# Column sums in 32-column tiles, roots spread by transposes, merge pairs in one PSUM bank, and single-tile stores at the end

## The chip, the cores and the metric

The kernel runs on one core of one Trainium2 chip. Its time is the device time of one execution in microseconds (us). Three runs of the kernel before took 1862.31, 1863.15 and 1863.52 us, a median of 1863.15 us. TensorE does the matrix products, VectorE the element work, ScalarE activations and copies, GpSimd a little of both; the SyncE queue issues the transfers. In the rows of the profile these are PE (with PEld for its weight loads), DVE, ACT, POOL and SP.

## The reference, cut to what matters

A sequence of 512 positions with 1024 features (fp32) goes through two blocks. Every layer starts with a norm over the features and adds its result to the stream `x`; in the first block the result of a layer is normed as well before it is added.

```python
def rmsnorm(x, g):
    return x * lax.rsqrt(jnp.mean(x * x, axis=-1, keepdims=True) + EPS) * g

# block 1
h = rmsnorm(x, norm_mix_pre); proj = h @ w_in
merged = sigmoid(g_a) * pool_mixer(u_pool) + sigmoid(g_b) * conformer_conv(u_glu)
x = x + rmsnorm(merged @ w_o, norm_mix_post)
f = square(relu(rmsnorm(x, norm_mlp_pre) @ w_up)) @ w_down
x = x + rmsnorm(f, norm_mlp_post)
# block 2
h = x + deltanet_mixer(rmsnorm(x, a_norm))      # 8 heads, chunks of 64, a triangular solve in each
h = h + conv_ffn(rmsnorm(h, f_norm[0]))
h = h + swa_sink_attention(rmsnorm(h, b_norm), kv)   # window 128, 16 heads
h = h + conv_ffn(rmsnorm(h, f_norm[1]))
return rmsnorm(h, final_norm)
```

## The kernel before

The stream lies in SBUF as 8 tiles of 128 features by 512 positions. Each big product is cut into blocks of 128x128 weights times 128x512; weights and inputs are split into a rounded fp32r part and a remainder, so that a block is three matmuls (`mm3`, L277 to L279). The weights come in units of 512 KB on the SyncE queue, ScalarE rounds them (L253) and VectorE forms the remainder (L254).

A norm needs the sum of squares over all features at each position. Features lie on partitions, so the squares of the 8 tiles are added up into one tile `sq`, and TensorE adds its 128 partitions: `colsum` (L341) takes each of the four 128-column blocks of `sq` as weights against a column of ones. The sums of 128 positions then stand on 128 partitions, one column for each block. `rms` (L373) scales them, takes the root by an integer guess and three Newton steps (`rsqrt`, L324, eleven small VectorE instructions with that scaling), and `bcast` (L348) spreads the four columns of roots along partitions again: VectorE multiplies the identity by each column (L352, four 128x128 diagonal matrices `dg`), and one matmul with ones (L355) writes the 128x512 result. `rms` is called seven times.

At three places a layer is handed to the next in two halves of the positions: between the mixer and the MLP of block 1, between that MLP and the delta layer, and from the last FFN to the final norm. `lin_split` (L405) computes the last 24 blocks of the outgoing product for the first 256 positions and then for the others, and `half_rms` (L436) is the norm of one half: two column sums (L440), the same root chain (L443, then L327 to L333), two diagonals (L447) and a 128x256 matmul (L449). `fold` (L427) adds the squares of each finished half tile to `sq`: ScalarE squares (L433), VectorE adds (L434). `begin` (L452) takes both halves' results `R`, updates the stream and splits it for the next product, and the first products of the next layer fill TensorE there. `final` (L1334) multiplies the halves by the roots (L1346, eight instructions of 128x256 a half) and stores pairs of tiles, 256 KB each, on the SyncE queue.

In the delta layer the heads' 64x64 triangular inverses are joined from 32x32 quarters for four heads at a time (`delta_merge`, L840, groups 0 and 1). One quarter step is many 32x32 or 64x64 matmuls that use only a part of the array: L867 first, then L882 with L883 into two PSUM tiles `p` and `r`, L888 into `r`, and for pairs of heads `left` (L898) into `pl` and `right` (L902) into `pr`; `right` needs the copy `M` of what `left` made of the same heads. These steps are woven between the blocks of other products (`weave`, L297).

The order on each engine is set by a scheduler at build time, from the order of the program, priorities and the tiles that are free. Each engine works its instructions strictly in that order. PSUM has eight banks: six or three for `acc`, two or five for `aux`, by stage.

Of the kernel before, what the change touches and what calls it, by code (L numbers as in the profile page):

```python
# [74 lines left out]
def _pack(i):  # L75
# [43 lines left out]
    for g, w in enumerate(WINDOWS):  # L119
        cnt[:, g * 16:g * 16 + w] = 1.0 / np.arange(1, w + 1, dtype=np.float32)  # L120
    a["cnt"] = cnt
# [69 lines left out]
class Net:  # L191
# [149 lines left out]
    def colsum(self, x):  # L341
        ps = self.aux()
        for b in range(NB):
            self.nc.tensor.matmul(ps[:, b:b + 1], lhsT=x[:, b * P:(b + 1) * P], rhs=self.ones[:, 0:1],
                                  start=True, stop=True)
        return ps[:, :NB]

    def bcast(self, y, copy=True):  # L348
        nc = self.nc
        dg = self.tmp()  # L350
        for b in range(NB):
            nc.vector.tensor_scalar(out=dg[:, b * P:(b + 1) * P], in0=self.ident, scalar1=y[:, b:b + 1],  # L352
                                    scalar2=None, op0=ALU.mult)
        ps = self.aux()
        nc.tensor.matmul(ps, lhsT=self.ones, rhs=dg, start=True, stop=True)  # L355
# [17 lines left out]
    def rms(self, acc, n, copy=True):  # L373
        v = self.small()
        self.nc.vector.tensor_scalar(out=v, in0=self.colsum(acc), scalar1=1.0 / n, scalar2=EPS,
# [60 lines left out]
    def half_rms(self, sq, i):  # L436
        nc = self.nc
        ps, h = self.aux(), S // 2
        for j in range(2):
            nc.tensor.matmul(ps[:, j:j + 1], lhsT=self.blk(sq, 2 * i + j), rhs=self.ones[:, 0:1],  # L440
                             start=True, stop=True)
        v = self.small(2)
        nc.vector.tensor_scalar(out=v, in0=ps[:, 0:2], scalar1=1.0 / D, scalar2=EPS, op0=ALU.mult, op1=ALU.add)  # L443
        y = self.rsqrt(v)
        dg = self.tmp()
        for j in range(2):
            nc.vector.tensor_scalar(out=self.blk(dg, j), in0=self.ident, scalar1=y[:, j:j + 1], scalar2=None,  # L447
                                    op0=ALU.mult)
        nc.tensor.matmul(ps[:, h:], lhsT=self.ones, rhs=dg[:, :h], start=True, stop=True)  # L449
        return ps[:, h:]  # L450

    def begin(self, gain, heads=()):  # L452
# [8 lines left out]
        for i in range(2):  # L461
            next(steps, None)
            R.append(self.half_rms(sq, i))
# [376 lines left out]
    def delta_merge(self, g):  # L840
# [38 lines left out]
        p, r = self.aux(), self.aux()  # L879
        for i in range(n):  # L880
            c = slice(i * Q, (i + 1) * Q)
            T.matmul(p[q[0], c], lhsT=TTq[q[1], i], rhs=Mq[q[1], i], start=True, stop=True)  # L882
            T.matmul(r[q[2], c], lhsT=Mq[q[3], i], rhs=TTq[q[3], i], start=True, stop=True)  # L883
        for k, t in enumerate(T64):
            A.copy(out=t[q[1], :, 0:Q], in_=half(cq(p)[q[0]], k))
        yield
        for i in range(n):
            T.matmul(r[q[0], i * Q:(i + 1) * Q], lhsT=Mq[q[1], i], rhs=TTq[q[1], i], start=True, stop=True)  # L888
        for i, s in enumerate(hs):
            for k, f in ((0, A.copy), (2, V.tensor_copy)):  # L890
                f(out=s["t4"][q[k], :, q[k + 1]], in_=cq(r)[q[k], i * NB:(i + 1) * NB])
# [12 lines left out]
        for h in range(0, GROUP + 2, 2):  # L904
            pl, pr = (self.aux() if h < GROUP else None), (self.aux() if h else None)
            for i in range(2 * NB):
                if h < GROUP:
                    left(h, i, c64(pl))
                if h:
                    right(h - 2, i, c64(pr))  # L910
            if h < GROUP:
                M = self.hid()
                A.copy(out=M[bot], in_=pl[top])
                Ms[h] = c64(M)
            if h:
                for i in range(2):
                    V.tensor_copy(out=hs[h - 2 + i]["t4"][top, :, bot], in_=c64(pr)[bot, i * NB:(i + 1) * NB])
# [188 lines left out]
    def ffn(self, i):  # L1106
# [23 lines left out]
        if i:  # L1130
            sq = self.tp.tile([P, S], F32, tag="sq", name=self.name("sq"), bufs=2)
# [6 lines left out]
            self.carry = self.lin_split(st, NH, hs, done), sq  # L1138
# [195 lines left out]
    def final(self):  # L1334
        nc = self.nc
        steps, sq = self.carry
# [55 lines left out]
```

## Time and profile before

| | |
|---|---|
| median of three runs | 1863.15 us |
| the profiled execution | 1860.65 us |
| its span, first to last instruction | 1858.7 us |
| mean granted TensorE clock | 0.992 |
| PE busy | 1825.9 us, 98% |
| DVE busy | 1232.8 us, 66% |
| ACT busy | 821.9 us, 44% |
| POOL busy | 94.3 us, 5% |
| DMA, mean over the span | 95 GB/s |

The durations below come from the profiled execution, whose time is 1.95 us over its span and 2.5 us under the median. A row of the timeline gives the start, how long the instruction or the run of like instructions lasted, engine, line, operation and operands. Matmuls overlap: a 128x512 block product lasts 0.39 us and the next starts 0.227 us after it, so that costs on TensorE are read from starts, not from durations. A column sum has its `sq` block as weights; a matmul of fp32 data shows as two records, a transpose as one.

### The profile page before, as it was taken

The numbers are of one execution on the slowest core, as the hardware profiler recorded it, in microseconds if no ns is written. First come the engines' busy times: TensorE is split into PE (matmuls) and PEld (weight loads), VectorE is DVE, ScalarE is ACT, GpSimd is POOL, SyncE is SP. The second block draws the span as 40 slices with busy tenths as digits, with TensorE's granted clock in tenths as the row PEclk, the third lists the DMA queues.
The fourth block names the chain that finished last, engine by engine and source line by source line (L and its number), as shares of the span: only waits on it lengthen the run. The fifth ranks groups of instructions, "written<-read, shape, count | busy, mean of one in ns | idle before, by whom it ended". The sixth has DMA issues, their size and how long they took to land.

```text
span 1858.7 us, 24170 instructions
## 1 busy us (share of the span) xinstructions
PE 1825.9 (98%) x9214; PEld 1517.8 (82%) x9214; DVE 1232.8 (66%) x2323; ACT 821.9 (44%) x1447; POOL 94.3 (5%) x225
## 2 busy tenths in 40 slices
PE   8999999999999999999999999999999999999997
PEld 6887898888888878787878888888877788888887
DVE  7999767423543887968687777633577777777334
ACT  5323443222332477755454444422377644444221
POOL 0000000000000026430000000000000000000000
PEclk9999999999999999999899999999999999999999
DMA  5322223323232322325123232222211222223221
GB/s 181 102 91 93 95 69 102 102 91 102 91 103 91 125 81 86 117 83 170 36 80 102 92 101 93 100 97 96 97 58 57 69 91 92 102 93 100 96 97 57
DMA packets 62676, 175.70 MB, mean 95 GB/s; under 512 B 15200, under 2 KB 17888, under 8 KB 62560
## 3 DMA queue, kind: packets, MB, share of 16 engines
q1 hardware_dynamic: 62560, 174.16, 28.3%
q8 instruction: 72, 1.18, 0.3%
q14 instruction: 44, 0.36, 0.1%
HBM read 166.80 MB, written 7.34 MB: 94 GB/s over the span
## 4 chain that ended last, share of the span: by engine, by line
PE 91%; DVE 7%; ACT 1%; issue 1%; DMA 0%; DVEq 0%; ACTq 0%
PE m L277 28%; PE m L278 28%; PE m L279 27%; DVE wl L254 1%; PE a L627 1%; PE a L1315 1%; PE a L641 1%; PE a L1255 1%; DVE t L616 1%; PE a L1308 1%; PE a L935 0%; DVE xl L312 0%; DVE h L1239 0%; PE a L355 0%; PE a L941 0%
## 5 line engine op out<-in xcount | busy, mean ns | idle before, releaser
L277 PE MATMUL m<-xh,wh 128*128 128x512 f32 (+1 forms) x1560 | 602.1, 389 | 10.9 <-ACT xh L311 6.6
L278 PE MATMUL m<-xl,wh 128*128 128x512 f32 (+1 forms) x1560 | 599.6, 385 | 0.6
L279 PE MATMUL m<-xh,wl 128*128 128x512 f32 (+1 forms) x1560 | 599.8, 385 | 0.2 <-DVE wl L254 0.2
L253 ACT CAST wh<-wr 128x1024 fp32r<-128x1024 f32 x302 | 317.0, 1051 | 570.7 <-PE m L278 473.6
L254 DVE TENSOR_TENSOR wl<-wr,wh 128x1024 fp32r<-128x1024 f32 x302 | 368.7, 1222 | 244.9 <-ACT wh L253 241.9
L277 PE MATMUL m<-h,wh 128*128 128x512 f32 (+1 forms) x972 | 360.8, 372 | 3.1 <-ACT h L308 2.3
L278 PE MATMUL m<-h,wh 128*128 128x512 f32 (+1 forms) x972 | 359.6, 370 | 0.0
L279 PE MATMUL m<-h,wl 128*128 128x512 f32 (+1 forms) x972 | 359.3, 370 | 0.0
L277 PEld LDWEIGHTS m<-xh,wh 128*128 128x128 f32 x1560 | 292.4, 189 | 71.8 <-ACT xh L311 9.4
L278 PEld LDWEIGHTS m<-xl,wh 128*128 128x128 f32 x1560 | 294.3, 189 | 59.4 <-DVE xl L312 2.5
L279 PEld LDWEIGHTS m<-xh,wl 128*128 128x128 f32 x1560 | 294.1, 189 | 57.6 <-issue 0.7
L277 PEld LDWEIGHTS m<-h,wh 128*128 128x128 f32 x972 | 183.6, 189 | 35.6 <-issue 3.1
L278 PEld LDWEIGHTS m<-h,wh 128*128 128x128 f32 x972 | 183.7, 189 | 30.9 <-issue 1.8
L279 PEld LDWEIGHTS m<-h,wl 128*128 128x128 f32 x972 | 183.6, 189 | 30.5 <-issue 0.6
L1119 DVE SCALAR_TENSOR_TENSOR t<-t,vecs,t 128x511 f32<-128x511 f32 (+1 forms) x176 | 131.2, 747 | 5.3 <-ACT t L1117 2.4
L1116 DVE TENSOR_TENSOR t<-m,R 128x512 f32<-128x512 f32 x88 | 60.5, 688 | 79.9 <-PE m L279 77.7
L308 ACT CAST h<-t 128x512 fp32r<-128x512 f32 x80 | 49.6, 621 | 139.6 <-DVE t L1127 115.1
L501 DVE SCALAR_TENSOR_TENSOR h<-h,vecs,h 128x511 f32<-128x511 f32 (+28 forms) x120 | 82.5, 731 | 0.9 <-ACT h L498 0.9
L309 DVE TENSOR_TENSOR h<-t,h 128x512 fp32r<-128x512 f32 x80 | 55.1, 689 | 28.4 <-ACT h L308 28.2
L1117 ACT ACTIVATE t<-t,vecs 128x512 f32<-128x512 f32 x88 | 71.5, 813 | 2.0 <-DVE t L1116 1.7
L1125 ACT ACTIVATE t<-t 128x512 f32<-128x512 f32 x44 | 27.8, 632 | 84.2 <-DVE t L1119 84.2
L583 DVE TENSOR_TENSOR t<-m,R 128x512 f32<-128x512 f32 x32 | 22.1, 690 | 58.6 <-PE m L279 56.7
(269 smaller groups left out, 1534.6 us busy)
## 6 DMA issues: line engine op xcount, KB each, us to landing
wr<-in_f_up SPq DMA_DIRECT2D x88, 512.0 KB, 3.5
wr<-in_f_down SPq DMA_DIRECT2D x44, 512.0 KB, 3.5
wr<-in_w_up SPq DMA_DIRECT2D x32, 512.0 KB, 3.5
wr<-in_w_down SPq DMA_DIRECT2D x32, 512.0 KB, 3.4
wr<-in_a_w_in SPq DMA_DIRECT2D x32, 512.0 KB, 3.5
wr<-in_w_in SPq DMA_DIRECT2D x28, 512.0 KB, 3.5
wr<-in_w_o SPq DMA_DIRECT2D x8, 512.0 KB, 3.5
spill<-h SPq DMA_DIRECT2D x16, 256.0 KB, 2.3
```

The costliest lines, as they stand in the source:

```text
L253: nc.scalar.copy(out=wh, in_=raw)
L254: nc.vector.tensor_tensor(out=wl, in0=raw, in1=wh.bitcast(F32), op=ALU.subtract)
L277: nc.tensor.matmul(ps, lhsT=w[0], rhs=x[0], start=start, stop=False)
L278: nc.tensor.matmul(ps, lhsT=w[0], rhs=x[1], start=False, stop=False)
L279: nc.tensor.matmul(ps, lhsT=w[1], rhs=x[0], start=False, stop=stop)
L308: nc.scalar.copy(out=hi, in_=src)
L309: nc.vector.tensor_tensor(out=lo, in0=src, in1=hi.bitcast(F32), op=ALU.subtract)
L501: nc.vector.scalar_tensor_tensor(out=c[:, d:], in0=v[:, :S - d], scalar=wt[CONV_K - 1 - d], in1=c[:, d:], op0=ALU.mult, op1=ALU.add)
L1116: V.tensor_tensor(out=u, in0=ps, in1=R, op=ALU.mult)
L1117: A.activation(out=y, in_=u, func=AF.Identity, scale=w[2], bias=self.vec(f"f_b{i}", c))
L1119: V.scalar_tensor_tensor(out=y[:, d:], in0=u[:, :S - d], scalar=w[2 - d], in1=y[:, d:], op0=ALU.mult, op1=ALU.add)
L1125: A.activation(out=g, in_=g, func=AF.Silu)
```

## The change

`colsum` takes each 128-column block as four tiles of 32 columns: 16 matmuls of 128x32 weights in place of four of 128x128, each writing its own 32 partitions of the result. It may also add up several input tiles. `spread` is new and replaces the diagonals and the matmul with ones: the column of roots, read as if repeated 128 times, is transposed by TensorE, one 128x128 transpose for each block of positions. Both serve `rms` and `half_rms`.

`root` is new and used by `half_rms` alone: ScalarE takes the square root of the scaled sum (L345 of the new program), VectorE inverts it (L347) and does one Newton step (L348 to L350). `rms` keeps `rsqrt`. In `delta_merge` the matmuls of `p` and `r` in the first step, and those of `left` and `right`, write different partitions of one PSUM tile; the copies move accordingly. In the last FFN the squares of the very last half tile go to a tile of their own, `rest`, and the column sum adds `sq` and `rest`. The final norm stores the second half in single tiles of 128 KB, in turn on the SyncE and the ScalarE queue.

```diff
+    def root(self, ps, n):
+        nc = self.nc
+        v, s, y, t = (self.small(ps.shape[1]) for _ in range(4))
+        nc.scalar.activation(out=s, in_=ps, func=AF.Sqrt, scale=1.0 / n, bias=self.cnt[:, 15:16])
+        nc.vector.tensor_scalar(out=v, in0=ps, scalar1=1.0 / n, scalar2=EPS, op0=ALU.mult, op1=ALU.add)
+        nc.vector.reciprocal(out=y, in_=s)
+        nc.vector.scalar_tensor_tensor(out=t, in0=y, scalar=-0.5, in1=y, op0=ALU.mult, op1=ALU.mult)
+        nc.vector.tensor_tensor(out=t, in0=t, in1=v, op=ALU.mult)
+        nc.vector.scalar_tensor_tensor(out=y, in0=t, scalar=1.5, in1=y, op0=ALU.add, op1=ALU.mult)
+        return y
+
-    def colsum(self, x):
+    def colsum(self, *xs, n=NB):
         ps = self.aux()
-        for b in range(NB):
-            self.nc.tensor.matmul(ps[:, b:b + 1], lhsT=x[:, b * P:(b + 1) * P], rhs=self.ones[:, 0:1],
-                                  start=True, stop=True)
-        return ps[:, :NB]
+        for b in range(n):
+            for i, x in enumerate(xs):
+                for g in range(0, P, Q):
+                    self.nc.tensor.matmul(ps[g:g + Q, b:b + 1], lhsT=x[:, b * P + g:b * P + g + Q],
+                                          rhs=self.ones[:, 0:1], start=i == 0, stop=i == len(xs) - 1)
+        return ps
+
+    def spread(self, ps, y):
+        for b in range(y.shape[1]):
+            self.nc.tensor.transpose(self.blk(ps, b), y[:, b:b + 1].to_broadcast([P, P]), self.ident)
+        return ps
...
+    def half_rms(self, i, *sqs):
+        y = self.root(self.colsum(*(t[:, HALVES[i]] for t in sqs), n=2)[:, 0:2], D)
+        return self.spread(self.aux(), y)[:, :S // 2]
...
-        p, r = self.aux(), self.aux()
+        p = self.aux()
         for i in range(n):
             c = slice(i * Q, (i + 1) * Q)
             T.matmul(p[q[0], c], lhsT=TTq[q[1], i], rhs=Mq[q[1], i], start=True, stop=True)
-            T.matmul(r[q[2], c], lhsT=Mq[q[3], i], rhs=TTq[q[3], i], start=True, stop=True)
+            T.matmul(p[q[2], c], lhsT=Mq[q[3], i], rhs=TTq[q[3], i], start=True, stop=True)
...
         for h in range(0, GROUP + 2, 2):
-            pl, pr = (self.aux() if h < GROUP else None), (self.aux() if h else None)
+            p = self.aux()
             for i in range(2 * NB):
                 if h < GROUP:
-                    left(h, i, c64(pl))
+                    left(h, i, c64(p))
                 if h:
-                    right(h - 2, i, c64(pr))
+                    right(h - 2, i, c64(p))
...
-                self.fold(sq, x, c, m == 0)
+                if m == NT - 1 and c == HALVES[1]:
+                    A.activation(out=rest[:, c], in_=x, func=AF.Square)
+                else:
+                    self.fold(sq, x, c, m == 0)
...
-            R = self.half_rms(sq, i)
+            R = self.half_rms(i, sq, rest) if i else self.half_rms(i, sq)
...
-                    if j % 2:
-                        nc.sync.dma_start(out=self.out[k + j - 1:k + j + 1, :, c].rearrange("k p s -> p k s"),
-                                          in_=t[:, j - 1:j + 1])
+                    if i:
+                        (nc.scalar if j % 2 else nc.sync).dma_start(out=self.out[m, :, c], in_=t[:, j])
+                    elif j % 2:
+                        nc.sync.dma_start(out=self.out[m - 1:m + 1, :, c].rearrange("k p s -> p k s"), in_=t[:, j - 1:j + 1])
```

The change also moves work in TensorE's order. The first place is the norm ahead of the attention (1320 us in the trace): `a` is the PSUM tile, `sq` the squares, L344 and L355 the old column sum and spread. In the kernel before thirteen block matmuls, of which the rows show the first two and the last, stood from one to the other:

```order
L279 MATMUL m_11253<-h_11154,wl_11256 128x512
L344 MATMUL a_11226<-ones,sq_11202 128x1 x4
L277 MATMUL m_11253<-h_11158,wh_11255 128x512
L278 MATMUL m_11253<-h_11159,wh_11255 128x512
...
L277 MATMUL m_11287<-h_11142,wh_11289 128x512
L355 MATMUL a_11249<-t_11244,ones 128x512
L278 MATMUL m_11287<-h_11143,wh_11289 128x512
```

The new column sum is L358 and the transposes of the roots `s` are L364; block matmuls are L278 to L280 there:

```order
L280 MATMUL m_11315<-h_11206,wl_11318 128x512
L358 MATMUL a_11278<-ones,sq_11254 32x1 x16
L278 MATMUL m_11315<-h_11210,wh_11317 128x512
L279 MATMUL m_11315<-h_11211,wh_11317 128x512
...
L279 MATMUL m_11315<-h_11219,wh_11317 128x512
L280 MATMUL m_11315<-h_11218,wl_11318 128x512
L364 MATMUL a_11308<-c_101,s_11296 128x128 x4
L278 MATMUL m_11349<-h_11190,wh_11351 128x512
```

The spread has moved up: nine block matmuls stand from the column sum to it, not thirteen. In the other six calls of `rms` the counts of rows are 16, 24, 18, 18, 18 and 13 before and 11, 17, 14, 14, 14 and 9 now.

The second place is the hand-over from the MLP to the delta layer (614 us), the first half. In the kernel before 23 block matmuls of 128x256 stood from the column sum L440 to the spread L449:

```order
L279 MATMUL m_4527<-h_3962,wl_4575 128x256
L440 MATMUL a_4674<-ones,sq_4122 128x1 x2
L277 MATMUL m_4527<-h_4001,wh_4574 128x256
...
L278 MATMUL m_4608<-h_3651,wh_4610 128x256
L449 MATMUL a_4674<-t_4691,ones 128x256
L279 MATMUL m_4608<-h_3650,wl_4611 128x256
```

The same place now:

```order
L280 MATMUL m_4559<-h_3994,wl_4607 128x256
L358 MATMUL a_4706<-ones,sq_4154 32x1 x8
L278 MATMUL m_4559<-h_4033,wh_4606 128x256
...
L278 MATMUL m_4559<-h_4150,wh_4606 128x256
L364 MATMUL a_4725<-c_101,s_4717 128x128 x2
L279 MATMUL m_4559<-h_4151,wh_4606 128x256
```

Ten stand there instead of 23, and the others come after the spread.

The third place is the merge of the second group of heads (882 to 891 us). L882 fills `p`, L883 and L888 fill `r`, L898 is `left`, L902 is `right`; before, from the first 32x32 step on:

```order
L882 MATMUL a_7856<-h_7784,h_7598 32x32 x12
L883 MATMUL a_7857<-h_7598,h_7784 32x32 x12
...
L888 MATMUL a_7857<-h_7598,h_7784 32x32 x16
L898 MATMUL a_7922<-h_7786,h_6338 64x64 x4
L898 MATMUL a_7922<-h_7786,h_6592 64x64 x4
L898 MATMUL a_7936<-h_7787,h_6961 64x64 x4
L898 MATMUL a_7936<-h_7787,h_7115 64x64 x2
L902 MATMUL a_7937<-h_6338,h_7931 64x64 x4
L902 MATMUL a_7937<-h_6592,h_7931 64x64 x2
```

Now L884 and L885 are the pair in one tile, L893 the later `r`, L902 `left` and L906 `right`:

```order
L893 MATMUL a_7941<-h_7641,h_7827 32x32 x11
L885 MATMUL a_7899<-h_7641,h_7827 32x32
L884 MATMUL a_7899<-h_7827,h_7641 32x32
...
L893 MATMUL a_7941<-h_7641,h_7827 32x32 x5
L278 MATMUL m_8087<-h_7876,wh_8089 128x512
L902 MATMUL a_7965<-h_7829,h_6382 64x64 x4
L902 MATMUL a_7965<-h_7829,h_6636 64x64 x4
L902 MATMUL a_7979<-h_7830,h_7004 64x64
L279 MATMUL m_8087<-h_7877,wh_8089 128x512
L280 MATMUL m_8087<-h_7876,wl_8090 128x512
L278 MATMUL m_8125<-h_7876,wh_8089 128x512
L906 MATMUL a_7979<-h_6382,h_7974 64x64
```

The two matmuls of a pair now take turns one by one through the whole step (fifteen times), and full-width block matmuls stand ahead of and between the `left` and `right` matmuls, where before none stood until the `right` ones were half done.

## Rows read from the trace of the kernel before

**Rows 1.** The page's fourth part: the chain that ended last, by engine.

```profile
PE 91%; DVE 7%; ACT 1%; issue 1%; DMA 0%; DVEq 0%; ACTq 0%
```

**Rows 2.** Stretches: length, busy time of the engines (instructions), granted clock, DMA.

```profile
20.00:222.00 202.00, 202.00 (x887) 164.84 (x886) 188.92 (x298) 74.11 (x96) 8.29 (x10) 1.00 0.29 96
252.00:282.00 30.00, 29.43 (x220) 27.27 (x220) 27.71 (x84) 17.29 (x34) 0.00 (x0) 1.00 0.16 54
611.00:642.00 31.00, 29.15 (x219) 26.98 (x218) 29.48 (x87) 17.91 (x34) 2.54 (x5) 1.00 0.34 120
792.30:795.50 3.20, 3.20 (x13) 2.18 (x13) 1.14 (x5) 1.76 (x5) 2.01 (x10) 0.50 0.02 5
884.40:897.90 13.50, 13.50 (x88) 11.66 (x86) 4.63 (x12) 5.21 (x14) 0.00 (x0) 0.50 0.01 2
```

**Rows 3.** Timeline of PE at the attention's norm: start, length, engine, line, operands.

```profile
1320.03 0.95 PE L344 MATMUL a<-ones,sq 128*128 128x1 f32 x8
1320.83 0.49 PE L277 MATMUL m<-h,wh 128*128 128x512 f32 x1
1321.16 0.40 PE L278 MATMUL m<-h,wh 128*128 128x512 f32 x1
...
1323.70 0.39 PE L277 MATMUL m<-h,wh 128*128 128x512 f32 x1
1324.12 1.12 PE L355 MATMUL a<-t,ones 128*128 128x512 f32 x2
1324.68 0.79 PE L278 MATMUL m<-h,wh 128*128 128x512 f32 x1
1325.31 0.40 PE L279 MATMUL m<-h,wl 128*128 128x512 f32 x1
```

**Rows 4.** Timeline of DVE there: first scaling, then the four diagonals.

```profile
1321.01 0.16 DVE L375 TENSOR_SCALAR s<-a 128x4 f32<-128x4 f32 x1 [1.27 <-PE a L344]
...
1323.18 0.88 DVE L352 TENSOR_SCALAR t<-c,s 128x128 f32<-128x128 f32 x4
```

**Rows 5.** Timeline of PE in the first merge.

```profile
785.07 1.20 PE L867 MATMUL a<-h,h 32*32 32x32 f32 x64
786.20 0.66 PE L627 MATMUL a<-c,h 128*128 128x128 f32 x4
786.61 0.47 PE L277 MATMUL m<-xh,wh 128*128 128x512 f32 x1
787.07 1.19 PE L882 MATMUL a<-h,h 32*32 32x32 f32 x32
788.20 0.50 PE L278 MATMUL m<-xl,wh 128*128 128x512 f32 x1
```

**Rows 6.** Timeline of PE at the hand-over to the delta layer.

```profile
615.55 0.70 PE L449 MATMUL a<-t,ones 128*128 128x256 f32 x2 [0.97 <-DVE t L447]
```

**Rows 7.** ScalarE's one-line operation on small tiles, and a table load.

```profile
L1271 ACT ACTIVATE s<-s x8: 198/208/212, 1359.8 to 1454.1; 128x8 f32<-128x8 f32 x8
L1271 ACT ACT_TABLE_LOAD  x1: 1283/1283/1283, 1358.5 to 1358.5; - x1
```

**Rows 8.** Timeline of PE in the second merge.

```profile
881.65 0.91 PE L882 MATMUL a<-h,h 32*32 32x32 f32 x23 [0.67 <-ACT h L869]
...
884.43 2.92 PE L898 MATMUL a<-h,h 64*64 64x64 f32 x25
```

**Rows 9.** The chain at the end, in order of time: start, length, what.

```profile
1847.31 0.44 DVE sq L434
...
1847.79 0.62 PE a L440 x4
...
1848.43 0.17 DVE s L443
...
1851.12 1.24 PE a L449 x2
...
1853.26 2.35 DVE o L1346 x6
```

More of the change, by code (lines that the diff above doesn't have):

```diff
@@ L339, in rsqrt @@
         return y
-    def colsum(self, x):
-        ps = self.aux()
-        for b in range(NB):
-            self.nc.tensor.matmul(ps[:, b:b + 1], lhsT=x[:, b * P:(b + 1) * P], rhs=self.ones[:, 0:1],
-                                  start=True, stop=True)
-        return ps[:, :NB]
+    def root(self, ps, n):
[9 more added lines that the diff above has]
+    def colsum(self, *xs, n=NB):
+        ps = self.aux()
+        for b in range(n):
[8 more added lines that the diff above has]
+        return ps
     def bcast(self, y, copy=True):
         nc = self.nc
[L350 to L355, printed above, removed]
+        ps = self.spread(self.aux(), y)
         if not copy:
@@ L434, in fold @@
         nc.vector.tensor_tensor(out=sq[:, c], in0=sq[:, c], in1=t[:, c], op=ALU.add)
[L436 to L450, printed above, removed]
+    def half_rms(self, i, *sqs):
+        y = self.root(self.colsum(*(t[:, HALVES[i]] for t in sqs), n=2)[:, 0:2], D)
+        return self.spread(self.aux(), y)[:, :S // 2]
     def begin(self, gain, heads=()):
@@ L882, in delta_merge @@
             T.matmul(p[q[0], c], lhsT=TTq[q[1], i], rhs=Mq[q[1], i], start=True, stop=True)
-            T.matmul(r[q[2], c], lhsT=Mq[q[3], i], rhs=TTq[q[3], i], start=True, stop=True)
+            T.matmul(p[q[2], c], lhsT=Mq[q[3], i], rhs=TTq[q[3], i], start=True, stop=True)
         for k, t in enumerate(T64):
             A.copy(out=t[q[1], :, 0:Q], in_=half(cq(p)[q[0]], k))
+        for i, s in enumerate(hs):
+            V.tensor_copy(out=s["t4"][q[2], :, q[3]], in_=cq(p)[q[2], i * NB:(i + 1) * NB])
         yield
+        r = self.aux()
         for i in range(n):
@@ L889, in delta_merge @@
         for i, s in enumerate(hs):
-            for k, f in ((0, A.copy), (2, V.tensor_copy)):
-                f(out=s["t4"][q[k], :, q[k + 1]], in_=cq(r)[q[k], i * NB:(i + 1) * NB])
+            A.copy(out=s["t4"][q[0], :, q[1]], in_=cq(r)[q[0], i * NB:(i + 1) * NB])
         yield
@@ L916, in delta_merge @@
                 for i in range(2):
[L917 removed]
+                    V.tensor_copy(out=hs[h - 2 + i]["t4"][top, :, bot], in_=c64(p)[bot, i * NB:(i + 1) * NB])
             yield
@@ L1130, in ffn @@
         if i:
-            sq = self.tp.tile([P, S], F32, tag="sq", name=self.name("sq"), bufs=2)
+            sq, rest = (self.tp.tile([P, S], F32, tag="sq", name=self.name("sq"), bufs=2) for _ in range(2))
             def done(m, ps, c):
@@ L1335, in final @@
         nc = self.nc
-        steps, sq = self.carry
+        steps, sq, rest = self.carry
         self.carry = None
```

12 lines of the change are left out of this document (7 added, 5 removed).

## The prediction

> **What bounds the kernel now.** I read the chain of waits first: 91% of the span is TensorE's, 7% VectorE's [rows 1]. So most of this change is worth what it takes out of TensorE's own stream, and VectorE's part counts only where TensorE stands for it. Next come the stretches [rows 2]. From 20 to 222 us TensorE is busy throughout, and VectorE 94% of the time. At the two hand-overs (252 to 282 and 611 to 642 us) TensorE is idle 0.57 and 1.85 us, and VectorE, at 92% and 95%, sets the pace. Two stretches run at a granted clock of 0.50, the lower level of 1.2 GHz: 3.2 us after the first merge and 13.5 us after the second. Last I read the timeline of one norm, of both merges, of one hand-over and of the end.
>
> **The seven calls of `rms`.** In the attention's norm the column sum starts at 1320.03, and the stream is regular again at 1325.31 [rows 3]: 5.28 us with 14 block matmuls in it. Between 1321.16 and 1323.70 eleven of them take 0.231 us each, so 14 are 3.23, and the norm costs TensorE 2.05 us. VectorE has the roots at 1323.18, 2.35 us after the column sum gave way at 1320.83, by eleven small instructions of 0.197 us each; then come the diagonals, 0.88 us, and the spread waits for them [rows 3, 4].
>
> The new column sum has 16 matmuls of 128x32, 32 records. No such shape occurs before. Its bounds are from the first merge [rows 5]: 64 records of 32x32 on two tiles in turn take 1.13 us (L867, 785.07 to 786.20), 0.018 a record; 32 on one tile take 1.13 too (L882), 0.035 a record. Two tiles at once would make it 0.57 us, four at once half of that, 0.28, one after another 1.13. I take 0.57, the measured rate of alternating tiles. Into the small tiles goes about 0.2 us more (the block matmul ahead of L882 takes 0.46 to the next start), and 0.1 after them.
>
> The Trainium skill ("TensorEngine Tiling (Array Packing)", Instruction Overhead) speaks against this edit: a matmul with one column takes as long as one with 60, and a dimension that is already small should give no tiling factor. By it 60 columns at the pace of a 512-column block are 0.027 us, 32 of them 0.87 us, and the whole sum below would be some 2 us smaller. L867's 0.018 a record, for 32 columns, does not bear that out where tiles take turns, so I keep 0.57.
>
> The four transposes take 0.41 us (L627, 786.20 to 786.61) [rows 5] where one fp32 matmul of 512 columns stood. They need no diagonals, but they need the roots, and they stand nine block matmuls behind the column sum, 2.08 + 0.1 us, where the roots take 2.35. So TensorE waits about 0.2 us, and the roots are loaded as weights in the wait, 0.1 (one transpose's pace). With 0.1 for the blocks' restart the new norm costs 0.2 + 0.57 + 0.1 + 0.2 + 0.1 + 0.41 + 0.1 = 1.68 us, 0.37 less than 2.05. The other calls lie alike: their spreads moved up to just where the roots come, whether 9, 14 or 17 rows, and what VectorE has queued between (a weight remainder) sets a wait of 0.2 to 0.5. Behind the waiting transposes the block matmuls are queued, and nobody else notices. Seven calls: 2.6 us. With four tiles at once it would be 7 x 0.66 = 4.6, with one after another 7 x -0.19 = -1.3.
>
> **The half norms in mid-kernel.** Five halves (the last one is below) have half the column sum and half the transposes; I take half of the saving, 0.2 each, 1.0 us, with bounds of -0.5 and 1.8. Beside it the gap of 0.97 us before L449 [rows 6] shrinks: ten matmuls of 128x256, 0.115 us each, now stand where 23 stood, so TensorE arrives after 1.2 us, while the new root takes a ScalarE square root, 0.21 us [rows 7], and four small VectorE instructions of 0.2, near 1.05, and the column sum's landing and the load before the first transpose another 0.4. About 0.3 of a wait stays: 0.65 us gained. VectorE loses six small instructions and two diagonals of 0.22 in each half, some 1 us, and sets the pace there [rows 2]; of the 1.45 us of TensorE's idle time that is left at both hand-overs I count half, 0.7. Against that, second halves have the spread 12 and 17 matmuls behind the column sum, and the root's five instructions lie between big VectorE ones there, so that a wait of up to 1 us each may come. Together 2.35 us, bounds -1.5 and 4.5. The table load of 1.28 us that comes with the square root [rows 7] falls twice into idle time of ScalarE, which has 17.29 us of work in 30 at the first hand-over [rows 2] and next to none near the end; uncovered it costs 1.28 each.
>
> **The merges.** In the first, L882, L883 and L888 use one tile each, 1.13 us a block [rows 5]; now the first two take turns (64 records at L867's rate, 1.13) and the third follows: 2.26 for 3.39, 1.1 less, and one switch of 0.2 less. In the second the three blocks already overlap a little, 2.78 us from 881.65 to 884.43 [rows 8]; 2.26 is 0.5 less. Sum 1.8. Behind them the clock is at half for 3.2 and 13.5 us [rows 2], and with block matmuls between the small ones some of that may come back: nothing at least, at most half of 16.7, 8.35. I take 1.6, a dip of the short kind. The sum is 3.4 us, bounds 1.0 and 10.
>
> The Trainium skill ("TensorEngine Tiling (Array Packing)", Gotcha 1: PSUM Pressure) says that different row tiles cannot access the same PSUM bank at once. Then a pair in one bank would run in series, 2.26 us for the first two blocks, and the merges would give only the clock's 1.6. L867 does write two tiles of one PSUM bank, at 0.018 us a record against L882's 0.035; the trace does not agree.
>
> **The end.** The addition L434 leaves the chain, 0.48 us (1847.31 to 1847.79). The column sum keeps its 0.64, since 12 of its 16 matmuls wait for `rest`. From 1848.43 to 1851.12, 2.69 us, stand the old root and the diagonals; the new root is 1.05: 1.64 less. L449 took 1.24 us; two transposes are 0.2 plus the 0.25 that the last of four lasts beyond the next start (0.66 against 0.41) [rows 5], up to twice that at half clock: 0.6, so 0.64 less, bounds 0.35 and 0.8. The eight multiplications stay (the last six 2.35 us, to 1855.61). The span ends 3.1 us after them; the last store is now 128 KB instead of 256 KB, on a queue of its own: 0.2 less, bounds 0 and 0.5. Sum 2.96 us, bounds 1.3 (a table load on the chain, no gain from the stores) and 3.5 [rows 7, 9].
>
> **Sum.** 2.6 + 2.35 + 3.4 + 2.96 = 11.3 us off the profiled execution's 1860.65, that is 1849.3; the median of the runs is 2.5 higher, so I forecast 1851.8, about 1852 (range of its own 1848 to 1856).
>
> **The rivals.**
> - *More comes back.* Four tiles run at once (2.0 more in `rms`, 0.7 in the halves) and half of the slow stretch returns (3 more): 1863.15 - 17 = 1846. For it: L867's tiles do overlap. Against: nothing before shows four.
> - *The 32-column tiles run one after another.* Then `rms` gives -1.3 instead of 2.6 and the halves lose 1.5: 11.3 - 5.4 = 5.9, 1857. For it: L882 alone took 0.035 a record. Against: L867.
> - *TensorE's savings turn into waits.* VectorE paces 20 to 222 us and the hand-overs [rows 2], the transposes stand for the roots, and the clock stays as it is: the end's 3.0 and 1.3 of the merges are left, 1859. For it: VectorE at 92% to 95%. Against: TensorE is never idle from 20 to 222 us.
> - *Slower, by the clock.* The rows at 0.50 follow blocks of small matmuls, and the change puts such a block into 13 norms, with a wait for the roots behind most. A dip like that at 792.3 costs 1.6 us; from seven such dips the gain is gone, and with ten it is 1863.15 - 11.3 + 16 = 1868. For it: two of two merges. Against: the blocks there last 1.1 us and come in a row, these 0.6 alone between full blocks.
>
> **Chances and range.** The forecast 0.52, more 0.14, one after another 0.17, waits 0.11, slower 0.06. 0.2% (3.7 us) is about what a measurement can tell from no change here: below 1859.4 fall the first two, nearly all of the third and half of the fourth, 0.83; 0.11 lie within, 0.06 above. The range, 1845 to 1860, takes in the first four down to a tenth of the better and the worse ones.
>
> **What will show it.** In the new profile: 16 column-sum matmuls from first to next block matmul in 0.6 to 0.7 us (0.4 with four at once, 1.2 in series); transposes within 0.5 us and a wait of 0.2 to 0.5 before them; no gap near 1 us at 614; the two paired steps of a merge in about 1.1 us; the stretch at half clock behind the second merge shorter than 13.5 us; the chain after the last block matmul some 3 us shorter. It is wrong if the column sums take over 1 us, if the clock dips at the norms, or if a table load stands on the chain.

## The result, and the profile after

The changed kernel took 1843.91 us (median of four runs, 1842.61 to 1847.29) against 1863.06 us (1862.31 to 1863.52) of the kernel before beside it: a ratio of 0.9896, interval 0.9884 to 0.9908, 19.2 us less. The forecast was 1852 with a range from 1845 to 1860: right in direction, too small, and the median is 1.1 us below the range. A second series of the same kernel (e5 below) gave 0.9904, interval 0.9890 to 0.9919. A profiled execution is one draw of its series: that of the kernel before is 2.4 us under its median, the first one of the changed kernel 3.4 us over its own (the slowest of the four) and e5's 1.1 under, so that differences of traces are smaller than the 19.2.

The two programs have the same 7632 block matmuls of `mm3`. Numbering them and subtracting the start of the k-th before from that of the k-th after shows where time was gained, since between the edits this difference stands still. Every column below is such a difference over a stretch, for the changed kernel's two traces (spans 1845.5 and 1841.8 us against 1858.7); the rows are rounded and add up to within 0.2 us:

| stretch | forecast | first trace | second (e5) |
|---|---|---|---|
| up to the first column sum | 0 | +2.6 | +2.6 |
| seven full norms | -2.6 | -5.9 | -5.9 |
| two hand-overs, first half of the last one | -2.35 | -5.4 | -5.4 |
| merges, 760 to 944 us | -3.4 | -1.75 | -7.1 |
| attention, 1343 to 1466 us | 0 | 0.0 | +1.6 |
| the end | -2.96 | -3.2 | -3.2 |
| from the scalars of the delta layer to 760 us | 0 | +0.35 | +0.33 |
| sum | -11.3 | -13.2 | -16.9 |

Norms, hand-overs and the end repeat to 0.1 us. Merges and attention don't; so a trace alone is no measure of the whole here. The forecast had no term for the start or the attention. Whether the later start is a loss of the edit is not shown: e11 below, which changes nothing ahead of 760 us, begins 1.2 us after the kernel before, e10 0.6, e8 1.4, and the other changed kernels 2.5 to 3.2.

The chain of the changed kernel, and its stretches (the answers to [rows 1, 2]):

```profile
PE 87%; DVE 6%; ACT 3%; issue 1%; DMA 1%; POOL 1%; SPq 0%; DVEq 0%; ACTq 0%
```

```profile
252.00:282.00 30.00, 29.11 (x254) 27.42 (x253) 26.65 (x70) 21.19 (x41) 0.00 (x0) 1.00 0.17 54
609.00:640.00 31.00, 29.73 (x251) 27.65 (x252) 29.39 (x73) 20.18 (x37) 3.54 (x5) 1.00 0.35 122
```

TensorE still holds the chain. At the hand-overs VectorE does its work with 70 and 73 instructions where it needed 84 and 87, and at the second TensorE stands idle 1.27 us instead of 1.85, though at the first 0.89 instead of 0.57. Somewhat more of the next products' blocks lie in the same stretch (the rows also count the column sums' extra records).

The timeline of TensorE at the attention's norm, after (columns as in [rows 3]; L358 is the column sum, L364 the transposes):

```profile
1312.20 0.39 PE L280 MATMUL m<-h,wl 128*128 128x512 f32 x1
1312.52 0.43 PE L358 MATMUL a<-ones,sq 128*32 128x1 f32 x32
1312.88 0.50 PE L278 MATMUL m<-h,wh 128*128 128x512 f32 x1
1313.22 0.39 PE L279 MATMUL m<-h,wh 128*128 128x512 f32 x1
...
1314.83 0.39 PE L280 MATMUL m<-h,wl 128*128 128x512 f32 x1
1315.22 0.65 PE L364 MATMUL a<-c,s 128*128 128x128 f32 x4
1315.63 0.48 PE L278 MATMUL m<-h,wh 128*128 128x512 f32 x1
1315.94 0.39 PE L279 MATMUL m<-h,wh 128*128 128x512 f32 x1
```

The 32 records pass in 0.36 us, 0.011 each, where [rows 5] had 0.018 as the quickest pace and [rows 3] a column sum of 0.80. Ahead of them 0.09 us is lost (1312.20 to 1312.52 instead of 0.23), and 0.16 ahead of the transposes (1314.83 to 1315.22). From 1312.52 to 1315.94 are 3.42 us with ten block matmuls (2.31): 1.11, with the 0.09 ahead 1.2 us for the norm, where 2.05 were spent before.

The hand-over to the delta layer, same view, where [rows 6] had a gap of 0.97 us:

```profile
610.42 0.28 PE L278 MATMUL m<-h,wh 128*128 128x256 f32 x1
610.64 0.41 PE L364 MATMUL a<-c,s 128*128 128x128 f32 x2
610.80 0.36 PE L279 MATMUL m<-h,wh 128*128 128x256 f32 x1
```

The transposes start 0.22 us after the block matmul ahead, which alone takes 0.12: 0.1 us of wait is left of 0.97. In the other three halves of the two hand-overs they start 0.12 to 0.23 us behind it.

The merges in the changed kernel's first trace, TensorE, with what ended a gap in brackets:

```profile
780.03 0.47 PE L278 MATMUL m<-xh,wh 128*128 128x512 f32 x1
782.05 0.24 PE L884 MATMUL a<-h,h 32*32 32x32 f32 x2 [1.55 <-ACT h L871]
782.23 0.66 PE L629 MATMUL a<-c,h 128*128 128x128 f32 x4
...
878.39 0.19 PE L885 MATMUL a<-h,h 32*32 32x32 f32 x1
878.39 0.19 PE L884 MATMUL a<-h,h 32*32 32x32 f32 x1
878.42 0.19 PE L885 MATMUL a<-h,h 32*32 32x32 f32 x1
...
883.69 0.63 PE L280 MATMUL m<-h,wl 128*128 128x512 f32 x1
884.12 0.63 PE L278 MATMUL m<-h,wh 128*128 128x512 f32 x1
```

and stretches of the same trace (columns as in [rows 2]):

```profile
755.00:779.00 24.00, 21.31 (x134) 17.47 (x134) 22.66 (x56) 17.70 (x45) 13.60 (x27) 1.00 0.46 131
782.80:789.30 6.50, 6.50 (x104) 5.84 (x104) 3.58 (x9) 5.00 (x22) 0.40 (x2) 0.51 0.19 75
878.50:888.50 10.00, 10.00 (x121) 7.75 (x115) 2.49 (x8) 3.67 (x10) 0.00 (x0) 0.50 0.03 10
```

In the first merge TensorE waits 1.55 us for ScalarE, and 6.5 us at half clock follow, 3.2 before [rows 2]; that is the loss that hides in the merges' -1.75. Behind the second, 10 us at half clock are left of 13.5. There a block matmul takes 0.43 us from start to start (883.69 to 884.12) where it takes 0.227 at full clock, so that a microsecond at half clock is about half a microsecond lost.

The end, all engines:

```profile
1836.26 0.24 PE L358 MATMUL a<-ones,sq 128*32 128x1 f32 x8
1836.37 0.42 DVE L1139 TENSOR_TENSOR h<-m,h 128x256 f32<-128x256 f32 x1 [1.08 <-PE m L280]
1836.83 0.42 ACT L1141 ACTIVATE sq<-h 128x256 f32<-128x256 f32 x1 [6.60 <-DVE h L1139]
1837.30 0.37 PE L358 MATMUL a<-ones,sq 128*32 128x1 f32 x24 [0.79 <-ACT sq L1141]
1837.74 0.26 ACT L345 ACTIVATE s<-a,c 128x2 f32<-128x2 f32 x1 [0.49 <-PE a L358]
1838.03 0.16 DVE L346 TENSOR_SCALAR s<-a 128x2 f32<-128x2 f32 x1 [1.24 <-ACT s L345]
...
1839.00 0.40 PE L364 MATMUL a<-c,s 128*128 128x128 f32 x2 [1.33 <-DVE s L350]
1839.44 3.22 DVE L1354 SCALAR_TENSOR_TENSOR o<-h,vecs,a 128x256 f32<-128x256 f32 x8 [0.59 <-PE a L364]
```

No addition stands between the square and the column sum. The root takes from 1837.74 to 1839.00, 1.26 us, where [rows 9] had 2.69 with the diagonals; VectorE's scaling (L346) starts only behind ScalarE's root, which the row names as what it waited for, though it needs the sums alone. The column sum takes 0.44 us (1837.30 to 1837.74) where L440 took 0.64, and the two transposes 0.44: they run at full clock, since it falls at 1841.1 here, where before it fell at 1850.3, ahead of L449. The span ends 2.84 us after the last multiplication (1842.66), 0.26 sooner than before.

### The profile page after: what moved, and what is told of

The parts are those of the page before. It is cut to its first block, busy times and chain, and to the rows that moved or that the text cites. A ratio compares the mean times of both kernels' runs of the same rounds, so it can differ in the third digit from the quotient of the medians.

```text
span 1845.5 us, 24647 instructions
## 1 busy us (share of the span) xinstructions
PE 1814.1 (98%) x9484; PEld 1508.4 (82%) x9484; DVE 1219.6 (66%) x2246; ACT 826.6 (45%) x1455; POOL 95.8 (5%) x225
## 4 chain that ended last, share of the span: by engine, by line
PE 87%; DVE 6%; ACT 3%; issue 1%; DMA 1%; POOL 1%; SPq 0%; DVEq 0%; ACTq 0%
PE m L278 27%; PE m L279 27%; PE m L280 27%; DVE wl L255 1%; DVE t L618 1%; PE a L1322 1%; PE a L1262 1%; ACT wh L254 1%; PE a L1315 0%; PE a L629 0%; DVE h L1269 0%; ACT h L1285 0%; DVE h L1246 0%; PE a L939 0%; PE a L945 0%
## 5 line engine op out<-in xcount | busy, mean ns | idle before, releaser
L278 PE MATMUL m<-xh,wh 128*128 128x512 f32 (+1 forms) x1560 | 602.1, 388 | 10.9 <-ACT xh L312 6.4
L280 PE MATMUL m<-xh,wl 128*128 128x512 f32 (+1 forms) x1560 | 599.7, 385 | 1.1 <-DVE wl L255 1.1
L278 PE MATMUL m<-h,wh 128*128 128x512 f32 (+1 forms) x972 | 360.8, 372 | 3.2 <-ACT h L309 2.3
L280 PE MATMUL m<-h,wl 128*128 128x512 f32 (+1 forms) x972 | 358.7, 369 | 0.0
L278 PEld LDWEIGHTS m<-xh,wh 128*128 128x128 f32 x1560 | 292.9, 189 | 70.9 <-ACT xh L312 9.3
L280 PEld LDWEIGHTS m<-xh,wl 128*128 128x128 f32 x1560 | 294.4, 189 | 58.7 <-DVE wl L255 2.0
L278 PEld LDWEIGHTS m<-h,wh 128*128 128x128 f32 x972 | 183.5, 189 | 35.2 <-ACT h L309 2.7
L280 PEld LDWEIGHTS m<-h,wl 128*128 128x128 f32 x972 | 183.6, 189 | 30.1 <-issue 0.4
L503 DVE SCALAR_TENSOR_TENSOR h<-h,vecs,h 128x511 f32<-128x511 f32 (+27 forms) x120 | 82.6, 732 | 1.0 <-ACT h L500 0.9
```

The lines of the kernel that those rows point to most:

```text
L278: nc.tensor.matmul(ps, lhsT=w[0], rhs=x[0], start=start, stop=False)
L280: nc.tensor.matmul(ps, lhsT=w[1], rhs=x[0], start=False, stop=stop)
L503: nc.vector.scalar_tensor_tensor(out=c[:, d:], in0=v[:, :S - d], scalar=wt[CONV_K - 1 - d], in1=c[:, d:], op0=ALU.mult, op1=ALU.add)
```

## The experiments

All are the changed kernel with one part altered, but e9 and e11, which start from the kernel before. Times are medians, ratios are to runs of the kernel before taken beside it. "Norms", "hand-overs", "merges" and "end" are differences to the first trace of the kernel before, as in the table above.

**e1, the tiles in turn or one by one.**

```diff
-        for b in range(n):
-            for i, x in enumerate(xs):
-                for g in range(0, P, Q):
+        for g in range(0, P, Q):
+            for b in range(n):
+                for i, x in enumerate(xs):
```

> The changed kernel, with the 16 column-sum matmuls of a norm in another order: all blocks of one 32-column tile, then those of the next. Theory (tiles run at once only when neighbours in the stream are on different tiles): 32 records go at the 0.035 us of L882 before, so about 1.1 us instead of 0.36, 7 x 0.75 + 6 x 0.37 = 7.5 us slower at most, some of it hidden in the second halves. Rival (a 32-column matmul with one column is short by itself, order does not matter): 0.36 us a sum again, no change in time.

1847.21 us, 0.9918 (0.9902 to 0.9935). The column sum in the timeline of its attention's norm:

```profile
1309.92 0.87 PE L358 MATMUL a<-ones,sq 128*32 128x1 f32 x32
1310.72 0.50 PE L278 MATMUL m<-h,wh 128*128 128x512 f32 x1
```

The same 32 records take 0.80 us, 0.025 each. The norms give 2.8 us instead of 5.9. So neighbours on different tiles do overlap, and the order is what makes the edit pay; but one tile by itself is quicker than the 0.035 of L882 that I had as the bound.

**e2, column sums over whole blocks.**

```diff
-                for g in range(0, P, Q):
-                    self.nc.tensor.matmul(ps[g:g + Q, b:b + 1], lhsT=x[:, b * P + g:b * P + g + Q],
+                if True:
+                    self.nc.tensor.matmul(ps[:, b:b + 1], lhsT=x[:, b * P:(b + 1) * P],
```

> The changed kernel with column sums of whole 128-column blocks as before, all else as changed. Theory (the term of the sum that was mis-sized is the column sum, 0.36 us and 0.1 around it instead of 0.81 and 0.1): 7 x 0.45 + 6 x 0.2 = 4.3 us slower. Rival (the extra gain comes from the earlier spread and the shorter wait, the column sum is worth what the prediction gave it): 1 to 2 us slower.

1847.20 us, 0.9922 (0.9907 to 0.9937). Norms -3.3 instead of -5.9, hand-overs -4.0 instead of -4.6, end -2.8 instead of -3.2. The column sum takes 0.81 us again:

```profile
1310.68 0.94 PE L358 MATMUL a<-ones,sq 128*128 128x1 f32 x8
1311.49 0.49 PE L278 MATMUL m<-h,wh 128*128 128x512 f32 x1
```

The theory holds: the 32-column tiles are worth 2.6 us in the seven full norms and about 1.2 more elsewhere, 3.8 of the 4.3 expected. My sum had given them 0.03 us a norm (0.80 + 0.1 before, 0.2 + 0.57 + 0.1 after).

**e3, diagonals in place of transposes.**

```diff
-        for b in range(y.shape[1]):
-            self.nc.tensor.transpose(self.blk(ps, b), y[:, b:b + 1].to_broadcast([P, P]), self.ident)
+        nc, dg, n = self.nc, self.tmp(), y.shape[1]
+        for b in range(n):
+            nc.vector.tensor_scalar(out=self.blk(dg, b), in0=self.ident, scalar1=y[:, b:b + 1], scalar2=None, op0=ALU.mult)
+        nc.tensor.matmul(ps[:, :n * P], lhsT=self.ones, rhs=dg[:, :n * P], start=True, stop=True)
```

> The changed kernel with the roots spread by diagonals and a matmul with ones as before, all else as changed. Theory (transposes save 0.45 us of TensorE and a wait of 0.1 a norm, and VectorE's diagonals, 0.44 a half, at the hand-overs and at the end): 7 x 0.55 + 4 x 0.4 + 1.2 = 6.6 us slower. Rival (the spread is hidden by the scheduler, which places it where the diagonals are ready): 3 us slower, all of it TensorE's own 0.45.

1851.82 us, 0.9948 (0.9933 to 0.9963). Norms -2.45 instead of -5.9, hand-overs -2.65 instead of -4.6, end -2.3 instead of -3.2: 6.2 us, as the theory had it. The timeline of the attention's norm:

```profile
1319.53 0.39 PE L278 MATMUL m<-h,wh 128*128 128x512 f32 x1
1319.92 1.13 PE L367 MATMUL a<-t,ones 128*128 128x512 f32 x2
1320.48 0.79 PE L279 MATMUL m<-h,wh 128*128 128x512 f32 x1
1321.12 0.40 PE L280 MATMUL m<-h,wl 128*128 128x512 f32 x1
```

The scheduler puts the matmul 13 block matmuls behind the sum again, and the wait ahead of it (0.39 from start to start) is the same 0.16 as with the transposes: they save the matmul, 1.2 us from 1319.92 to 1321.12 less one block, against 0.72 from 1315.22 to 1315.94 less one block.

**e4, the merge as before.** `delta_merge` is the old one, everything else changed.

```diff
-        p = self.aux()
+        p, r = self.aux(), self.aux()
...
-            p = self.aux()
+            pl, pr = (self.aux() if h < GROUP else None), (self.aux() if h else None)
```

> The changed kernel with the merge of the delta layer as before (pairs in two PSUM tiles). Theory (the traces give the merges a net of 1.4 us, of which the second merge won 2.4 and the first lost 1.6 by a new wait of 1.55 us and a longer half-clock stretch, a dip at 765 us away from the merges being left out): 0 to 2 us slower, with the wait before the first pair gone. Rival (the merge gave the 3.4 us of the prediction, and the clock's dips fall by chance): 3 us or more slower.

1851.81 us, 0.9946 (0.9931 to 0.9961). The rival was nearer: by the ratios 8 to 9 us slower than the changed kernel's two series, though not measured beside either. In its trace the merges lose 2.5 us against the first trace of the kernel before, and 13.7 us at half clock lie behind the second merge, in this stretch of 16 (10.2 more lie in the first merge):

```profile
881.00:897.00 16.00, 16.00 (x146) 14.02 (x142) 5.30 (x15) 6.18 (x18) 0.00 (x0) 0.57 0.01 3
```

The wait before the first pair is there too, 1.28 us: it does not belong to the new order. Nothing else moved (norms -5.8, hand-overs -4.6).

**e5, the changed kernel once more.** No edit.

> The changed kernel once more, for its own scatter. Theory (the trace of the first run was an unlucky one: a wait of 1.55 us before the first pair of the first merge, then 6.8 us at half clock, where the kernels with another column sum had neither): about 0.9900 of the time before, single times spread over 4 us, and where the trace has no such wait, less than 13.7 us at half clock behind the two merges. Rival (the wait belongs to the changed order): the same wait and the same 6.8 and 10.2 us again.

1844.67 us (1843.60 to 1846.95), 0.9904 (0.9890 to 0.9919). The theory held: no wait in the first merge, and the merges give 7.1 us. Three stretches of its trace:

```profile
758.00:766.00 8.00, 6.03 (x16) 4.88 (x17) 6.37 (x18) 5.54 (x16) 1.22 (x7) 0.58 0.37 131
877.00:883.00 6.00, 6.00 (x66) 4.70 (x62) 0.90 (x4) 2.48 (x8) 0.00 (x0) 0.72 0.00 1
1444.50:1449.00 4.50, 4.01 (x18) 3.43 (x20) 2.64 (x9) 2.73 (x7) 0.00 (x0) 0.62 0.00 0
```

Half clock falls at other places: 6.8 us behind the gap at 757, where the first trace had none (1.00 from 755 to 779), nothing in the first merge, only 3.4 us behind the second, and 3.4 in the attention, the +1.6 of the table. In the thirteen traces of this study the first merge has a wait of 1.3 to 1.55 us just in the four (after, e3, e4, e7) without a half-clock stretch near 760; in the nine with one it has none. What ScalarE copies ahead of that pair comes from a transfer, as in the first trace:

```profile
775.92 0.61 ACT L878 COPY h<-h 32x128 f32<-32x128 f32 x2 [1.51 <-DMA h<-scr]
```

ScalarE waits for it 1.23 to 1.51 us in the four traces and 0.71 to 1.02 in the nine. So TensorE seems to pay at one place or at the other: where it lost no time near 760 it comes before the transfer's data and waits. No run tests this.

**e6, old roots in the half norms.**

```diff
-        y = self.root(self.colsum(*(t[:, HALVES[i]] for t in sqs), n=2)[:, 0:2], D)
+        v = self.small(2)
+        self.nc.vector.tensor_scalar(out=v, in0=self.colsum(*(t[:, HALVES[i]] for t in sqs), n=2)[:, 0:2],
+                                     scalar1=1.0 / D, scalar2=EPS, op0=ALU.mult, op1=ALU.add)
+        y = self.rsqrt(v)
```

> The changed kernel with the old root chain (integer guess and three Newton steps, eleven small VectorE instructions) in the six half norms; column sums, transposes and the end as changed. Theory (VectorE sets the pace at the hand-overs, and the end is a pure chain): 1.1 us more at the end, 0.6 a half at the hand-overs, 3 to 3.5 us slower than the changed kernel. Rival (the hand-overs gain by TensorE's savings alone): 1.1 us slower, all of it at the end.

1846.46 us, 0.9912 (0.9898 to 0.9927), in its trace hand-overs -2.8 instead of -4.6, last first half -0.6 instead of -0.8, end -2.0 instead of -3.2. That is 3.3 us, as the theory said, though the times show 1.8. The last transposes stand for the old chain 2.35 us, where the new root let them wait 1.33:

```profile
1838.91 0.66 PE L364 MATMUL a<-c,s 128*128 128x128 f32 x2 [2.35 <-DVE s L334]
```

The end and the hand-overs both pay in the trace, so the rival is out; the intervals of the times overlap. Some 0.25 us of the end's loss is the clock, which here falls before these transposes, and at the hand-over to the delta layer 0.43 us is TensorE's own wait for the longer chain.

**e7, the old end.** `ffn` and `final` as before, but for the call of `half_rms`: the last squares are added up by VectorE, and pairs of tiles are stored on the SyncE queue.

```diff
-                    if i:
-                        (nc.scalar if j % 2 else nc.sync).dma_start(out=self.out[m, :, c], in_=t[:, j])
-                    elif j % 2:
+                    if j % 2:
```

> The changed kernel with the old end: the last squares added by VectorE into one tile, pairs of tiles stored by the SyncE queue. Theory (the addition is 0.45 us of the chain, the smaller last stores 0.2): 0.6 us slower, below what the times can tell; the trace shows it from the last block matmul to the end. Rival (single-tile stores on two queues save the larger part of the landing): 1.5 us or more.

1846.50 us, 0.9911 (0.9896 to 0.9926), an interval that overlaps e5's. The trace decides: end -2.5 instead of -3.2, 0.75 us. In its chain the addition is back:

```profile
1836.97 0.42 ACT t L447
...
1837.42 0.44 DVE sq L448
```

It is 0.44 us of the 0.75, the rest is the stores' 0.3; the rival's 1.5 is out.

**e8, the new root in the full norms too.**

```diff
-        v = self.small()
-        self.nc.vector.tensor_scalar(out=v, in0=self.colsum(acc)[:, :NB], scalar1=1.0 / n, scalar2=EPS,
-                                     op0=ALU.mult, op1=ALU.add)
-        y = self.rsqrt(v)
+        y = self.root(self.colsum(acc)[:, :NB], n)
```

> The changed kernel with the new root in the seven full norms too, which brings seven more table loads on ScalarE. Theory (TensorE waits 0.15 us for the roots in six norms, and VectorE loses six small instructions in each): 1 us faster at most, 7 x 0.15, if the table loads of 1.28 us are hidden. Rival (in the full norms ScalarE has squares and weight casts in its queue, so the root comes later, not sooner): 1 to 5 us slower, with longer waits before the transposes.

1841.70 us (1839.52 to 1842.31), 0.9885 (0.9869 to 0.9902): the lowest median of all; its runs lie below all of e5's beside it, though the intervals of the two ratios overlap. Norms -6.9 instead of -5.9, and 1 us more between 656 and 760 us. At the attention's norm:

```profile
1307.78 0.39 PE L280 MATMUL m<-h,wl 128*128 128x512 f32 x1
1308.01 0.60 PE L364 MATMUL a<-c,s 128*128 128x128 f32 x4
```

The wait of 0.16 us ahead of the transposes is gone. The rest of the 3 us lies in the start and the merges, which scatter, so the traces show 2 us of it, less 0.5 that the end lost. The theory's 1 us is what the norms gave; the 1 us between 656 and 760 us it did not foresee, and its cause is not shown.

**e9, the kernel before once more.** No edit.

> The kernel before once more, for its own scatter. Theory (its first trace was a lucky one: it began about 2 us sooner than those of the changed kernels and had no half-clock stretch near 1445 us, and its timed runs lie 2.4 us over it): starts near 24 us where the first column sum stood at 21.4, perhaps a stretch of 3.4 us at half clock in the attention, and 13.7 us at half clock behind the second merge again. Rival (these are the changed kernel's own losses): the same trace as the first one.

1862.64 us, 0.9992 (0.9983 to 1.0001). The rival: its start is the first trace's within 0.2 us, and all norms, hand-overs, the attention and the end are the same within 0.1 us. So the later start and the stretch near 1445 us in the attention do not come from a lucky first trace of the kernel before. Nine of the ten traces with the changed norms have that stretch (all but the first; it starts at 1443 to 1456 us), and none of the three with the old ones (before, e9, e11): it looks like a loss of the change, 1.6 us, but no run shows which part brings it. Only the clock differs in e9, with no stretch at half clock behind the first merge and 17.1 us of it behind the second:

```profile
880.00:899.00 19.00, 18.67 (x186) 16.67 (x187) 6.75 (x17) 7.09 (x19) 0.00 (x0) 0.55 0.06 24
```

**e10, only `left` and `right` in one bank.** The first 32x32 step keeps `p` and `r`.

```diff
-        p = self.aux()
+        p, r = self.aux(), self.aux()
...
-            T.matmul(p[q[2], c], lhsT=Mq[q[3], i], rhs=TTq[q[3], i], start=True, stop=True)
+            T.matmul(r[q[2], c], lhsT=Mq[q[3], i], rhs=TTq[q[3], i], start=True, stop=True)
```

> The changed kernel with only left and right in one PSUM bank; the first 32x32 step writes two banks as before. Theory (the half-clock stretch behind the second merge shortens because block matmuls now stand between the left and right matmuls): at most 10.2 us at half clock there, time within 1.5 us of the changed kernel, the 0.5 us of the first step lost. Rival (it shortens because the 32x32 steps take turns on two tiles): 13.7 us again and 3 us or more slower than the changed kernel.

1847.54 us, 0.9924 (0.9910 to 0.9937), and behind the second merge 6.8 us at half clock:

```profile
877.00:886.00 9.00, 9.00 (x135) 7.73 (x131) 2.30 (x7) 3.20 (x9) 0.00 (x0) 0.62 0.05 20
```

So in this trace `left` and `right` among block matmuls are enough to shorten that stretch. By the ratios the time is some 4 us above the changed kernel's, though (0.9924 against 0.9904), more than the 1.5 expected: in the trace 6.8 us at half clock stand in the first merge, as in the changed kernel's first trace but without a wait ahead. And with the half-clock time counted at half, the merges' own saving is nearly gone here, some 1.5 us (an estimate) and not 0.5.

**e11, the merge alone on the kernel before.** The reverse of e4's edit, on the kernel before:

```diff
-        p, r = self.aux(), self.aux()
+        p = self.aux()
...
-            pl, pr = (self.aux() if h < GROUP else None), (self.aux() if h else None)
+            p = self.aux()
```

> The kernel before with the new merge of the delta layer alone. Theory (the merge is worth 5 to 7 us, most of it clock: e4, the changed kernel without it, lost 7 to 8): 5 to 7 us faster than before, 3.4 to 10.2 us at half clock behind the second merge. Rival (its gain needs the shifts in the norms ahead of it): 2 us faster or less, 13.7 us at half clock.

1856.65 us, 0.9963 (0.9951 to 0.9976), 6.2 us faster; in the trace the merges give 5.0 us and nothing else moves (norms -0.2, hand-overs and end 0.0). Behind the second merge 6.8 us at half clock are left:

```profile
882.00:891.00 9.00, 9.00 (x144) 7.42 (x142) 1.92 (x6) 2.80 (x9) 0.00 (x0) 0.62 0.02 8
```

The half-clock time behind the second merge, read in stretches of 0.5 us: old merge 13.7 (before), 17.1 (e9), 13.7 us (e4); new merge 10.2, 6.8, 6.8, 6.8, 3.4, 6.8, 6.8 and 6.8 us (after, e1, e2, e3, e5, e6, e7, e8), and 6.8 in e10 and e11. No trace of one kind, three and ten of them, reaches the other.

## Why the prediction was too small

Three terms of the sum were mis-sized, all too low: the column sum, the half norms and the clock behind the merges.

**The seven norms: the step that failed is "I take 0.57, the measured rate of alternating tiles".** The column sum takes 0.36 us, because four tiles overlap, where L867 in [rows 5] had only two to alternate. The mechanism of my rival "more comes back" is what happened, and e1 and e2 show it from both sides; its own 1846 us was still 2 too high. Two smaller terms of the same sum were too dear as well: 0.2 us to get into the tiles (0.09), and 0.3 of wait and load ahead of the transposes (0.16). Together 0.48 us a call, 3.3 us over seven, which is what the norms gave beyond the forecast. The transposes at 0.41 us were right to 0.01, and so was the wait's existence. The Trainium skill's rule ("TensorEngine Tiling (Array Packing)", Instruction Overhead) would have led further away: by my estimate from it 0.027 us a record, against 0.011 measured with neighbours on other tiles. Its number fits only e1, where they are on one tile (0.025).

**The half norms: "I take half of the saving" failed.** The first half of the last hand-over, where TensorE alone counts, gained 0.79 us, not 0.2. A half has half the records, but the old form's wait for the diagonals (0.28 us ahead of L449 at 1841.23 before, none now) and its switches were whole. Of the hand-overs' 4.6 us the experiments give 0.6 to the column sums (e2), 1.95 to the transposes (e3) and 1.8 to the root (e6). The remaining wait I put at 0.3 is 0.1, and the waits of up to 1 us that I feared in the second halves did not come (14 and 17 block matmuls stand there in the trace; I had 12 and 17). That VectorE sets the pace there fits e6, which gives back 1.8 us when only VectorE's chain grows, of which 0.43 us shows as TensorE's wait for the roots.

**The merges: "I take 1.6, a dip of the short kind" failed; TensorE's own part was right.** I forecast 1.8 us of TensorE's own work and 1.6 of clock. From 740 to 944 us the kernel before runs 20.5 us at half clock, the changed kernel's first trace 17.1, e5 10.2 and e11 13.7. With half of the difference put down to the clock (1.7, 5.1 and 3.4 us) and the wait of 1.55 taken out of the first trace, 1.6, 1.95 and 1.6 us are left for TensorE's own work, an estimate that bears out the 1.8. The timed runs agree that the clock is the larger part: the granted clock on record has a mean of 0.9906 in the fifteen runs of the kernel before beside e11 and of 0.9944 in e11's five, which over 1857 us is 7 us, an estimate good to about 1 us, where 6.2 were measured. I had bounded the clock's part (up to 8.35) but took the short dip's value without a reason that the rows gave. A price by the Trainium skill's rule on row tiles and banks ("TensorEngine Tiling (Array Packing)", Gotcha 1: PSUM Pressure) is not seen here: the pair in one bank runs on two tiles in turn at 0.03 us for two records in the second merge (878.39 to 878.42), until the clock falls, and in two banks it ran at that pace before:

```profile
883.12 0.19 PE L882 MATMUL a<-h,h 32*32 32x32 f32 x1
883.12 0.19 PE L883 MATMUL a<-h,h 32*32 32x32 f32 x1
883.15 0.19 PE L882 MATMUL a<-h,h 32*32 32x32 f32 x1
```

Whether two tiles write one bank at the same instant these rows do not tell, in the prediction's L867 either.

**The end was close:** 3.2 us for 2.96. The root cost 1.26, not 1.05, because the scaling waits for ScalarE's root; the transposes cost 0.44, not 0.6; the column sum gave 0.2, for which I had nothing; the stores gave 0.26 for 0.2. So the total is close partly by misses that cancel.

**The rivals.** Tiles one after another: refuted by the 0.36 us, and priced by e1. Savings turned into waits: the full norms kept all they saved, in the stretch where VectorE is 94% busy too (-0.94 and -0.81 us in its two norms). Slower by the clock: in the changed kernel's first trace no stretch at half clock follows any of the 13 column sums but the very last, where one stood before.

**What stays open** is why half clock falls where it does from one execution to the next (760, 783 or 1445 us in the same program), which moves one run by 1.7 us a stretch of 3.4 us, and whether the later start and the stretch in the attention, for which the sum had no term, belong to the change: the traces give 13.2 and 16.9 us with the start, 15.8 and 19.5 without it.

## What to carry to other kernels

For matmuls with a single moving column, cutting the weights into 32-column tiles paid here because neighbours in the stream sit on different tiles: 0.36 us for a sum that took 0.80 whole, and 0.80 again with the tiles in the wrong order. When a form is priced from the trace, its fixed parts (the wait ahead, the switch) must be priced apart from what scales. Where the clock drops behind blocks of small matmuls, spreading them among full ones can be worth more than the time that the small ones take out (e11: 3.4 us of its trace's 5.0), and one trace is too few to say how much.

## What the runs showed of the hardware

- 16 fp32 matmuls of 128x32 weights and one column pass at 0.011 us a record on four tiles in turn, 0.025 on one tile after another; four of 128x128 take 0.10 a record (0.80 for eight).
- In this program VectorE's scaling starts 0.03 us after ScalarE's root of the same column sums has ended (1837.74 + 0.26, then 1838.03), after 1.24 us of idling. The row names the root as what it waited for; whether it could start sooner was not tried.
- At half clock a block matmul of 128x512 takes 0.43 us from start to start, at full clock 0.227.
- The two table loads of the root in the changed kernel's first trace (252.6 and 1828.7 us) do not stand on its chain, and in e8 none of the seven does.
